# A two-layer decoder trunk on one core: the order of the mixers' side work changed

## The chip, the core and the metric

The kernel runs on one NeuronCore of a Trainium2 chip. TensorE (PE) multiplies matrices and writes PSUM; VectorE (DVE), ScalarE (ACT) and GpSimd (POOL) do elementwise work; SyncE (SP) issues the transfers from HBM. Each engine works through its own instruction list strictly in order and waits for semaphores of the others. The metric is the device time of one execution in microseconds (us).

## The reference

A trunk of two layers over x of 256 × 2048, in fp32:

```python
# each layer, h = x @ w_in split by columns
y = concat(hgrn2(q, f, i, g), nsa(q, k_c, v_c, k_s, v_s, k_w, v_w, gate))
x = layer_norm(alpha * x + y @ w_out)
x = layer_norm(alpha * x + conv_ffn(x))        # w_up, causal conv of 3, silu gate, w_down

def compress(kv, pe, w1, w2):                  # of k_c and of v_c
    blk = kv[:, :, idx] + pe                   # 15 blocks of 32 positions, step 16
    return silu(flat(blk) @ w1) @ w2
# nsa: compressed, selected and sliding attention of 16 heads in 4 groups, summed with gates
# hgrn2: a gated linear recurrence of 8 heads with a state of 128 x 128, then RMS norm, gate
```

## The kernel before, in words

**Units.** All weights stream through one list of units (`run`). A unit is one transfer of 512 KB or 280 KB into one of 5 raw buffers, a split of each weight into a high part (whi, by ScalarE, or by GpSimd from the twentieth unit of a layer on: `POOL = 20`) and a low part (wlo = raw − whi, by VectorE), and matmuls. Transfers are issued up to 7 units ahead, splits are made up to 3 ahead, 4 buffers each for whi and wlo. A w_in or w_out unit is 8 blocks of two matmuls (512 columns with whi, 256 with wlo); a unit of w_vg, the values and gates of the selected and sliding branches, is 12 matmuls of 280 columns; a compression unit is 8 matmuls of 256 columns with w_c1 taken raw.

**The order of a layer's units** is written out in the mixer: three pairs of w_in columns (compressed, selected and window keys; `pairs(0, 3)`), the keys' eight vg units with a compression unit behind each two, the pair of the compressed values (vc), the same for the values, and then q, f, g and v units by a plan string, w_out, w_up, w_down.

**Side work.** Attention and the recurrence are generators in two queues, `att` and `hgr`. `pump` takes a step of one or the other after each unit. `cmp_in` (8 instructions of VectorE) lays out the compression's input from the keys or the values, plus a position term; `cmp_tail` does silu and the second product. Keys reach `cmp_in` through `total` (the sum of both halves in PSUM), a swap of halves (L400, 4 instructions) and two sums (L402, L403). The keys of the windows are also split for the scores, kh by ScalarE and kl by VectorE (L432). The scores of a query (L513) wait for its q, split at L413. `pre_att`, ahead of the first block of w_out, ends all that is left in the attention queue.

**What sets the final order.** A scheduler places the recorded instructions on each engine; the names end in numbers of buffers.

Of the kernel before, what the change touches and what calls it, by code (L numbers as in the profile page):

```python
# [29 lines left out]
F32 = mybir.dt.float32  # L30
# [11 lines left out]
KT = D // 128  # L42
# [23 lines left out]
VG = 280  # L66


def blocks(cts, nk, outer=0, head=0, tail=0):

    first, rest = cts[:outer], cts[outer:]
    if head:
        o = [(c, k) for c in first for k in range(head)]
        o += [(c, k) for c in first for k in range(head, nk)]
    else:
        o = [(c, k) for k in range(nk - tail) for c in first]
        o += [(c, k) for c in first for k in range(nk - tail, nk)]
    return o + [(c, k) for c in rest for k in range(nk)]  # L80
# [2 lines left out]
N_IN = 40  # L83
OUTER, TAIL = 6, 2
ORDER_IN = blocks(range(N_IN), KT, outer=OUTER, tail=TAIL)
ORDER_OUT = blocks(range(KT), KT, outer=3, head=12)
ORDER_UP = blocks(range(2 * FT), KT, outer=OUTER, tail=TAIL)
ORDER_DOWN = blocks(range(KT), FT)

# [3 lines left out]
RAW_BUFS, PART_BUFS = 5, 4  # L93
LOOK_DMA, LOOK_SPLIT = 7, 3
URGENT = 4
POOL = 20

AFTER = 3, 5, 6, 8, 9, 10, 12, 13, 14
# [5 lines left out]
class Trunk:  # L104
    def __init__(self, tc, a):
        self.tc, self.nc, self.a = tc, tc.nc, a
        self.side = self.att = deque()
        self.side2 = self.hgr = deque()
        self.n = 0
        self.scopes = {}  # L110
        self.barriers, self.last = deque(), None
        self.back = iter(())


    def nm(self, s):
# [24 lines left out]

    def pump(self, k):

        while k > 0 and (self.side or self.side2):
            q = self.side if self.side else self.side2
            try:
                next(q[0])
                k -= 1
            except StopIteration:
                q.popleft()
                continue  # L150
            self.side, self.side2 = self.side2, self.side
# [285 lines left out]
    def cmp_in(self, l, kv, src):  # L437


        F = self.scratch()[:, :960].rearrange("p (j n) -> p j n", j=16)  # L440
        pe = self.par[:, P_PE + 32 * kv:P_PE + 32 * kv + 32]
        for g in range(4):
            r = 64 * (g % 2)
            for hf in range(2):
                b = src[r:r + 64, g // 2, 16 * hf:16 * hf + 240].rearrange(
                    "p (n j) -> p j n", n=NCMP)
                self.nc.vector.tensor_add(  # L447
                    F[64 * hf:64 * hf + 64, :, g * NCMP:g * NCMP + NCMP], b,
                    pe[r:r + 64, 16 * hf:16 * hf + 16].unsqueeze(2).to_broadcast([64, 16, NCMP]))
        return F  # L450

    def cmp_tail(self, l, kv, ps):
        nc, mw, n = self.nc, self.mw, 4 * NCMP
        t2 = self.t(mw, [128, 2, S], F32, "rope2")
        hd, sg = t2[:, 0], t2[:, 1]
        nc.scalar.activation(hd[:n], ps[64:64 + n, :256], AF.Copy)
        nc.vector.tensor_add(hd[:n], ps[:n, :256], hd[:n])
        nc.scalar.activation(sg[:n], hd[:n], AF.Sigmoid)
        nc.vector.tensor_mul(sg[:n], hd[:n], sg[:n])
        hT = self.t(mw, [128, 128], F32, "AD")[:, :2 * n].rearrange("p (k n) -> p k n", k=2)  # L460
        pt = self.t(self.ps_t, [128, 512], F32, "t")
        for k in range(2):
            nc.tensor.transpose(pt[:, k * n:k * n + n], sg[:n, k * 128:k * 128 + 128],
                                self.ident[:n, :n])
        nc.scalar.activation(hT.rearrange("p k n -> p (k n)"), pt[:, :2 * n], AF.Copy)
        po = self.t(self.ps_s, [128, 512], F32, "s")
        if kv == 0:
            for k in range(2):
                nc.tensor.matmul(po[:, :n], self.par[:, P_W2K + k * 128:P_W2K + k * 128 + 128],
                                 hT[:, k], start=k == 0, stop=k == 1)  # L470
            pv = po[:, :n].rearrange("p (g n) -> p g n", g=4)
            nc.scalar.activation(self.kh[:, :, :NCMP], pv, AF.Copy)
            nc.vector.tensor_sub(self.kl[:, :, :NCMP], pv, self.kh[:, :, :NCMP].bitcast(F32))
        else:
            for g in range(4):
                for k in range(2):
                    r = 32 * (g % 2)
                    nc.tensor.matmul(po[r:r + NCMP, g * 64:g * 64 + 64],
                                     hT[:, k, g * NCMP:g * NCMP + NCMP],
                                     self.par[:, P_W2V + k * 64:P_W2V + k * 64 + 64],  # L480
                                     start=k == 0, stop=k == 1, skip_group_check=True)
            for h in range(2):
                src = po[32 * h:32 * h + NCMP, :256].rearrange("p (j c) -> p j c", j=2)
                for r in (32 * h, 64 + 32 * h):
                    nc.scalar.activation(self.vcmp[r:r + NCMP, :, self.gc(0, h)],
                                         src[:, :, self.gc(0, h)], AF.Copy)
# [229 lines left out]
    def hgrn_out(self, l, hp, g):  # L716
# [4 lines left out]
        for h in range(2):  # L721
            c = slice(256 * (hp % 2) + 128 * h, 256 * (hp % 2) + 128 * h + 128)
# [21 lines left out]
        for h in range(2):  # L744
# [1 line left out]
            v.scalar_tensor_tensor(ov[:, h], pt[:, h].rearrange("p t c -> p (t c)"),  # L746
                                   self.par[:, P_NW + hh:P_NW + hh + 1], g["g"][:, h],
                                   op0=ALU.mult, op1=ALU.mult)
        if hp > 1:
            self.open_o(4 + hp)  # L750
        o = self.o[4 + hp]
        act(o[:, :, 0], ov, AF.Copy)
# [262 lines left out]
    def open_mix(self):  # L1015
# [1 line left out]

        self.mo, self.o = mo, [None] * 8
        self.pad = self.t(mo, [128, 16], F32, "pad")
        for p in range(6):  # L1020
            self.open_o(p)
        self.P = (self.t(mo, [128, 2, 2, 2, 128], F32, "o6")[:, 0],
                  self.t(mo, [128, 2, 2, 2, 128], F32, "o7"))
# [15 lines left out]
    def layer(self, l):  # L1039
        a, nc = self.a, self.nc  # L1040
# [29 lines left out]
        def d_q(j, ip):  # L1070
            def f(t):
                q = self.q_in(t)
                for i in range(2):
                    self.att.append(self.attend(j, 2 * ip + i, q[:, i]))
            return f

        hg = [dict() for _ in range(4)]
# [43 lines left out]
        def cmp_units(kv):  # L1121
            st = {}
            out = []
            for c in range(4):
                def cb(raw, c=c):
                    if c == 0:
                        st["ps"] = self.t(self.ps_h, [128, 512], F32, "h")
                    F = box[f"F{kv}"]
# [4 lines left out]
                                         raw[:, k * 256:k * 256 + 256],  # L1133
                                         start=jj < 2, stop=jj > 13, skip_group_check=True)
                    if c == 3:
                        self.cmp_tail(l, kv, st["ps"])
                out.append((a["w_c1"][l, kv, c], 1024, False, cb, LOOK_SPLIT))
            return out

# [41 lines left out]
        def pairs(p, n=1):  # L1181
            return tiles[4 * p:4 * (p + n)]
# [1 line left out]
        def values(n):  # L1184
            return self.tok_units(lambda kq: a["w_v"][l, n, kq], 512, 2, d_hv(n), pump=2)

        u = pairs(0, 3)
        for br in range(2):
            if br:
                u += pairs(3)  # L1190
            vg = self.tok_units(lambda kq, br=br: a["w_vg"][l, br, kq], VG, 2, d_vg(br))
            for c, cu in enumerate(cmp_units(br)):
                u += vg[2 * c:2 * c + 2] + [cu]
        Q, F, G = 4, 8, 10
        for step in PLAN.split():
            n = int(step[1])
# [6 lines left out]
            else:  # L1203
# [1 line left out]

        u[POOL:] = [x + (True,) for x in u[POOL:]]
        u += self.units(lambda n: a["w_out"][l, n], ORDER_OUT, lambda k: self.o[k // 2][:, k % 2], KT, self.d_res(l, 0),
                        pre={(0, 0): pre_att, (0, 8): pre_hgr, (0, 12): pre_out}, last=KT - 1)
        u += self.units(lambda n: a["w_up"][l, n], ORDER_UP, xin, KT, self.d_ff(l),
                        pre={(0, 0): pre_up}, wide=OUTER, group=8)  # L1210
        u += self.units(lambda n: a["w_down"][l, n], ORDER_DOWN, lambda k: self.f[:, k], FT,
# [131 lines left out]
```

## Time and profile before

| | |
|---|---|
| three runs | 2509.39, 2510.86, 2510.89 us; median 2510.86 |
| the profiled execution | 2509.09 us |
| its span, first to last instruction | 2507.3 us |
| PE, DVE, ACT, POOL busy | 98%, 71%, 48%, 17% |
| matmuls of w_in, w_up, w_down, w_out | most of PE's time |
| transfers | 432 MB read, 173 GB/s over the span |

PE is the engine that sets the span: what does not make PE wait costs nothing. A wait in the views below is idle time of an engine, with the instruction that ended it. Two of PE's matmuls that follow without a wait start a fixed time apart, so a stretch's own work can be counted from such starts.

### The profile page before, as it was taken

Reading aid. Unit: us, or ns where it says so; the run is one execution under the profiler, and the core shown is the slowest. Engines: PE = TensorE matmul, PEld = TensorE weight load, DVE = VectorE, ACT = ScalarE, POOL = GpSimd, SP = SyncE. Lnnn points to the kernel's source line nnn. Section 1 sums busy time; section 2 is a strip of 40 time slices with the busy share of each in tenths; the row PEclk is TensorE's granted clock in tenths of the full one; section 3 lists DMA queues with packets and bytes.
Section 4 is the critical chain, followed back from the end, with each engine's and each line's share of the span. In section 5 each row is a group of like instructions: output and inputs, shape, how many; then the busy total and the mean of one; then the engine's idle time right before and its main releaser. Section 6 shows DMA issues by size and latency. Waiting matters only on the chain.

```text
span 2507.3 us, 41290 instructions
## 1 busy us (share of the span) xinstructions
PE 2451.8 (98%) x15993; PEld 2116.0 (84%) x15993; DVE 1780.8 (71%) x2705; ACT 1196.0 (48%) x2189; POOL 428.0 (17%) x403
## 2 busy tenths in 40 slices
PE   8999999999999999999989999999999999999997
PEld 7788877888888888888878888788888888888887
DVE  7767876787777777555597678766977777775554
ACT  4144425465555555334331444354655555553443
POOL 0444551300000000001014445513000000000011
PEclk9999999999999999999999999999999999999999
DMA  6644343556666555566546443445556565566562
GB/s 236 213 155 142 119 145 124 184 163 193 192 193 190 190 192 192 187 193 193 160 155 204 159 135 124 139 134 177 174 190 192 192 191 189 192 187 197 181 201 101
DMA packets 122884, 436.99 MB, mean 174 GB/s; under 512 B 13760, under 2 KB 14528, under 8 KB 122688
## 3 DMA queue, kind: packets, MB, share of 16 engines
q1 hardware_dynamic: 122688, 434.35, 54.0%
q8 instruction: 126, 2.06, 0.3%
q14 instruction: 70, 0.57, 0.1%
HBM read 432.20 MB, written 2.10 MB: 173 GB/s over the span
## 4 chain that ended last, share of the span: by engine, by line
PE 86%; DVE 8%; issue 2%; POOL 1%; ACT 1%; DMA 1%; SPq 0%; ACTq 0%; POOLq 0%; DVEq 0%
PE pj L325 49%; PE pj L328 26%; DVE wlo L238 3%; PE pj L322 1%; PE t L325 1%; DVE rope L400 1%; PE pj L365 1%; PE pj L364 1%; PE pj L363 1%; PE h L657 1%; DVE sg L447 1%; PE s L592 1%; POOL whi L235 1%; DMA raw<-w_in 1%; PE s L513 1%
## 5 line engine op out<-in xcount | busy, mean ns | idle before, releaser
L238 DVE TENSOR_TENSOR wlo<-raw,whi 128x1024 fp32r<-128x1024 f32 (+2 forms) x819 | 1019.3, 1246 | 534.9 <-ACT whi L237 447.0
L325 PE MATMUL pj<-x,whi 128*128 128x512 f32 x3904 | 1117.6, 395 | 8.5 <-ACT whi L237 4.6
L237 ACT ACTIVATE whi<-raw 128x1024 fp32r<-128x1024 f32 (+2 forms) x631 | 661.9, 1049 | 788.8 <-PE pj L325 598.3
L325 PEld LDWEIGHTS pj<-x,whi 128*128 128x128 f32 x3904 | 709.0, 188 | 139.7 <-ACT whi L237 4.6
L328 PE MATMUL pj<-x,wlo 128*128 128x256 f32 x3904 | 715.6, 281 | 2.6 <-DVE wlo L238 2.5
L328 PEld LDWEIGHTS pj<-x,wlo 128*128 128x128 f32 x3904 | 592.2, 188 | 38.1 <-DVE wlo L238 4.0
L325 PE MATMUL pj<-f,whi 128*128 128x512 f32 x1320 | 329.7, 392 | 0.0
L235 POOL TENSOR_SCALAR whi<-raw 128x1024 fp32r<-128x1024 f32 (+1 forms) x188 | 218.1, 1162 | 329.3 <-PE pj L325 122.9
L325 PEld LDWEIGHTS pj<-f,whi 128*128 128x128 f32 x1320 | 235.9, 188 | 40.6
L828 POOL TENSOR_TENSOR s<-z 128x512 f32<-128x512 f32 x4 | 6.8, 1706 | 1179.3 <-DVE z L825 1179.3
L328 PEld LDWEIGHTS pj<-f,wlo 128*128 128x128 f32 x1408 | 188.0, 188 | 13.6
L328 PE MATMUL pj<-f,wlo 128*128 128x256 f32 x1408 | 192.9, 278 | 0.0
L1000 DVE SCALAR_TENSOR_TENSOR ct<-ch,par,ct 128x255 f32<-128x255 f32 (+1 forms) x352 | 168.0, 481 | 5.6
L325 PE MATMUL pj<-o,whi 128*128 128x512 f32 x480 | 169.9, 396 | 1.9 <-DVE o L600 1.9
L328 PE MATMUL pj<-o,wlo 128*128 128x256 f32 x512 | 144.1, 283 | 0.0
L325 PEld LDWEIGHTS pj<-o,whi 128*128 128x128 f32 x480 | 90.1, 188 | 23.8 <-DVE o L600 2.4
L998 ACT ACTIVATE ct<-ch,par 128x256 f32<-128x256 f32 x176 | 103.0, 588 | 0.0
L328 PEld LDWEIGHTS pj<-o,wlo 128*128 128x128 f32 x512 | 96.2, 188 | 0.4
L364 PE MATMUL pj<-wlo,x 128*128 128x280 f32 (+1 forms) x256 | 90.9, 356 | 4.9 <-DVE wlo L238 4.8
L363 PE MATMUL pj<-whi,x 128*128 128x280 f32 (+1 forms) x256 | 89.7, 357 | 2.7 <-POOL whi L235 2.7
L365 PE MATMUL pj<-whi,x 128*128 128x280 f32 (+1 forms) x256 | 90.5, 356 | 0.0
L375 DVE TENSOR_TENSOR ch<-pj,ch 128x256 f32<-128x256 f32 x170 | 70.9, 418 | 3.0 <-ACT ch L374 3.0
(248 smaller groups left out, 2244.8 us busy)
## 6 DMA issues: line engine op xcount, KB each, us to landing
raw<-w_up SPq DMA_DIRECT2D x352, 512.0 KB, 4.3
raw<-w_down SPq DMA_DIRECT2D x176, 512.0 KB, 4.1
raw<-w_in SPq DMA_DIRECT2D x158, 512.0 KB, 3.8
raw<-w_out SPq DMA_DIRECT2D x64, 512.0 KB, 3.6
raw<-w_v SPq DMA_DIRECT2D x32, 512.0 KB, 3.8
raw<-w_vg SPq DMA_DIRECT2D x32, 280.0 KB, 3.0
raw<-w_c SPq DMA_DIRECT2D x16, 512.0 KB, 3.6
out<-z SPq DMA_DIRECT2D x3, 512.0 KB, 2.6
```

Of the source, the lines that this page charges most:

```text
L235: self.nc.gpsimd.tensor_scalar(hi, raw, 1.0, 0.0, op0=ALU.mult, op1=ALU.add)
L237: self.nc.scalar.activation(hi, raw, AF.Copy)
L238: return self.nc.vector.tensor_sub(lo, raw, hi.bitcast(F32))
L322: mm(out[:, 0], hi[:, o], x[:, p], start=k == 0 and p == 0, stop=False, skip_group_check=True)
L325: mm(out, hi[:, o], x, start=k == 0, stop=False, skip_group_check=True)
L328: mm(st[c][:, 0], lo[:, 128 * i:128 * i + 128], act(k)[:, 0], start=False, stop=k == nk - 1, skip_group_check=True)
L363: mm(st[tt], xh, wh, start=first, stop=False, skip_group_check=True)
L364: mm(st[tt], xh, wl, start=False, stop=False, skip_group_check=True)
L365: mm(st[tt], xl, wh, start=False, stop=kt == KT - 1, skip_group_check=True)
L375: self.nc.vector.tensor_add(out, ps[:, 0], out)
L998: act(t[:, c], h[:, c], AF.Identity, scale=w[2], bias=w[3])
L1000: v.scalar_tensor_tensor(t[:, c, s:], h[:, c, :S - s], w[n], t[:, c, s:], op0=ALU.mult, op1=ALU.add)
```

## The change

Five edits, all to the mixers. (1) The pair vc comes directly behind the other three pairs; the vg and compression units of the keys and of the values then follow each other without a break. With that the twentieth unit of a layer, from which GpSimd splits, is the keys' fourth vg unit. (2) `cmp_in` of the values writes a buffer with the tag "o5" instead of the scratch that the keys' input uses; the sixth attention output, which has that tag too, is opened later. (3) `cmp_tail` is a generator: its first step runs at once, the rest is queued in `att` and may start two ticks (calls of `pump`) later. (4) An attention job put into an empty queue may start six ticks later. (5) The first three columns of w_out are taken in blocks of six, six and four tiles, and `pre_att` stands ahead of the seventh tile.

```diff
@@ -66,14 +66,13 @@
-def blocks(cts, nk, outer=0, head=0, tail=0):
+def blocks(cts, nk, outer=0, head=(), tail=0):
     if head:
-        o = [(c, k) for c in first for k in range(head)]
-        o += [(c, k) for c in first for k in range(head, nk)]
+        o = [(c, k) for a, b in zip((0, *head), (*head, nk)) for c in first for k in range(a, b)]
     else:
@@ -83,7 +82,7 @@
 ORDER_IN = blocks(range(N_IN), KT, outer=OUTER, tail=TAIL)
-ORDER_OUT = blocks(range(KT), KT, outer=3, head=12)
+ORDER_OUT = blocks(range(KT), KT, outer=3, head=(6, 12))
 ORDER_UP = blocks(range(2 * FT), KT, outer=OUTER, tail=TAIL)
@@ -93,6 +92,7 @@
 URGENT = 4
+DELAY = 6
 POOL = 20
@@ -110,6 +110,7 @@
         self.back = iter(())
+        self.ticks, self.due, self.kept = 0, {}, []
@@ -140,8 +141,14 @@
+        self.ticks += 1
+        early = lambda q: bool(q) and self.due.get(id(q[0]), 0) > self.ticks and k < 1 << 10
         while k > 0 and (self.side or self.side2):
-            q = self.side if self.side else self.side2
+            if early(self.side) and not self.side2 or early(self.side2) and not self.side:
+                return
+            q = self.side if self.side and not early(self.side) else self.side2
+            if not q or early(q):
+                return
             try:
@@ -437,7 +444,8 @@
-        F = self.scratch()[:, :960].rearrange("p (j n) -> p j n", j=16)
+        F = (self.t(self.mo, [128, 1024], F32, "o5") if kv else self.scratch())[:, :960]
+        F = F.rearrange("p (j n) -> p j n", j=16)
         pe = self.par[:, P_PE + 32 * kv:P_PE + 32 * kv + 32]
@@ -450,6 +458,7 @@
     def cmp_tail(self, l, kv, ps):
         nc, mw, n = self.nc, self.mw, 4 * NCMP
@@ -457,12 +466,14 @@
         nc.vector.tensor_mul(sg[:n], hd[:n], sg[:n])
+        yield
         hT = self.t(mw, [128, 128], F32, "AD")[:, :2 * n].rearrange("p (k n) -> p k n", k=2)
         nc.scalar.activation(hT.rearrange("p k n -> p (k n)"), pt[:, :2 * n], AF.Copy)
+        yield
         po = self.t(self.ps_s, [128, 512], F32, "s")
@@ -746,7 +757,7 @@
                                    op0=ALU.mult, op1=ALU.mult)
-        if hp > 1:
+        if hp > 0:
             self.open_o(4 + hp)
@@ -1017,7 +1028,7 @@
         self.pad = self.t(mo, [128, 16], F32, "pad")
-        for p in range(6):
+        for p in range(5):
             self.open_o(p)
@@ -1071,7 +1082,12 @@
                 for i in range(2):
-                    self.att.append(self.attend(j, 2 * ip + i, q[:, i]))
+                    job = self.attend(j, 2 * ip + i, q[:, i])
+                    if not self.att:
+                        self.due[id(job)] = self.ticks + DELAY
+                        self.kept.append(job)
+                    self.att.append(job)
             return f
@@ -1133,7 +1149,11 @@
                     if c == 3:
-                        self.cmp_tail(l, kv, st["ps"])
+                        job = self.cmp_tail(l, kv, st["ps"])
+                        next(job)
+                        self.att.append(job)
+                        self.due[id(job)] = self.ticks + 2
+                        self.kept.append(job)
                 out.append((a["w_c1"][l, kv, c], 1024, False, cb, LOOK_SPLIT))
@@ -1184,10 +1204,8 @@
-        u = pairs(0, 3)
+        u = pairs(0, 4)
         for br in range(2):
-            if br:
-                u += pairs(3)
             vg = self.tok_units(lambda kq, br=br: a["w_vg"][l, br, kq], VG, 2, d_vg(br))
@@ -1205,7 +1223,7 @@
         u += self.units(lambda n: a["w_out"][l, n], ORDER_OUT, lambda k: self.o[k // 2][:, k % 2], KT, self.d_res(l, 0),
-                        pre={(0, 0): pre_att, (0, 8): pre_hgr, (0, 12): pre_out}, last=KT - 1)
+                        pre={(0, 6): pre_att, (0, 8): pre_hgr, (0, 12): pre_out}, last=KT - 1)
         u += self.units(lambda n: a["w_up"][l, n], ORDER_UP, xin, KT, self.d_ff(l),
```

TensorE at the keys' compression in layer 0, before (h is the compression's sum, sg the laid-out input, pj_106 and pj_107 the two halves of vg):

```order
L363 MATMUL pj_106_545<-whi_121_628,x_7_73 128x280
L363 MATMUL pj_107_546<-whi_121_628,x_7_73 128x280
L1132 MATMUL h_112_579<-raw_72_351,sg_97_470 60x256 x4
L1132 MATMUL h_112_579<-raw_93_437,sg_97_470 60x256 x4
L1132 MATMUL h_112_579<-raw_108_559,sg_97_470 60x256 x4
L364 MATMUL pj_106_545<-wlo_122_629,x_7_73 128x280
L365 MATMUL pj_106_545<-whi_121_628,x_7_73 128x280
```

And now, from the first compression on, and then from the third on (pj_121 and pj_122 are the halves of vg):

```order
L370 MATMUL pj_121_648<-whi_124_664,x_7_73 128x280
L1148 MATMUL h_127_682<-raw_97_478,sg_96_469 60x256 x4
L1148 MATMUL h_127_682<-raw_112_590,sg_96_469 60x256 x4
L371 MATMUL pj_121_648<-wlo_125_665,x_7_73 128x280
L372 MATMUL pj_121_648<-whi_124_664,x_7_73 128x280
```

```order
L1148 MATMUL h_127_682<-raw_123_662,sg_96_469 60x256 x4
L1148 MATMUL h_127_682<-raw_131_705,sg_96_469 60x256 x4
L370 MATMUL pj_122_649<-whi_109_567,x_7_73 128x280
L371 MATMUL pj_122_649<-wlo_110_568,x_7_73 128x280
L372 MATMUL pj_122_649<-whi_109_567,x_7_73 128x280
```

The second half of vg, which used to alternate with the first, now stands behind all four compressions and writes pj_122.

VectorE there, before (hz and rope are the keys in work, kl the low part of the window keys):

```order
L447 TENSOR_TENSOR sg_97_470<-hz_96_455,par_75_357 64x16x15 x8
L238 TENSOR_TENSOR wlo_122_629<-raw_111_577,whi_121_628 128x560
L432 TENSOR_TENSOR kl_28_128<-rope1_99_485,kh_27_127 64x2x2x128 x2
L238 TENSOR_TENSOR wlo_125_647<-raw_113_584,whi_124_646 128x560
L432 TENSOR_TENSOR kl_28_128<-rope1_99_485,kh_27_127 64x2x2x128 x2
L375 TENSOR_TENSOR rope1_101_515<-t_40_153,rope1_101_515 128x256
L375 TENSOR_TENSOR rope1_101_515<-t_41_156,rope1_101_515 128x256
L400 TENSOR_TENSOR rope2_102_524<-rope1_101_515,cf32_77_361 32x512 x4
L238 TENSOR_TENSOR wlo_129_671<-raw_119_620,whi_128_670 128x1024
```

And now (h_127 is the sum of the keys' compression, pj_107 one half of the compressed values):

```order
L410 TENSOR_TENSOR rope1_100_488<-rope1_100_488,rope2_101_497 128x512
L455 TENSOR_TENSOR sg_96_469<-hz_95_454,par_74_356 64x16x15 x8
L245 TENSOR_TENSOR wlo_125_665<-raw_108_565,whi_124_664 128x560
L439 TENSOR_TENSOR kl_27_127<-rope1_100_488,kh_26_126 64x2x2x128 x4
L382 TENSOR_TENSOR rope1_102_518<-t_39_152,rope1_102_518 128x256
L382 TENSOR_TENSOR rope1_102_518<-t_40_155,rope1_102_518 128x256
L407 TENSOR_TENSOR rope2_103_527<-rope1_102_518,cf32_76_360 32x512 x4
L409 TENSOR_TENSOR rope1_102_518<-rope1_102_518,cf32_76_360 128x512
L410 TENSOR_TENSOR rope1_102_518<-rope1_102_518,rope2_103_527 128x512
L439 TENSOR_TENSOR kl_27_127<-rope1_102_518,kh_26_126 64x2x2x128 x4
L466 TENSOR_TENSOR rope2_149_818<-h_127_682,rope2_149_818 60x256
L382 TENSOR_TENSOR rope1_111_587<-pj_107_548,rope1_111_587 128x256
```

The splits (wlo) that stood between the kl instructions are gone from there; the sum from the keys' compression and the total of the compressed values (pj_107) stand behind the window keys instead.

TensorE at the start of w_out in layer 0, before (t_681 turns the recurrence's output, t_702 the last attention job's probabilities):

```order
L325 MATMUL pj_718_4584<-o3_21_119,whi_697_4473 128x512
L328 MATMUL pj_718_4584<-o3_21_119,wlo_698_4474 128x256
L739 MATMUL t_681_4381<-cf32_77_361,rope2_679_4372 128x128 x4
L572 MATMUL t_702_4480<-cf32_77_361,P0_640_4130 128x128
L573 MATMUL t_702_4480<-cf32_77_361,P1_639_4129 128x128
```

And now (s_677 are scores, t_673 turns the recurrence's output, s_685 collects an attention job):

```order
L548 MATMUL s_677_4334<-cb_77_362 128x288
L750 MATMUL t_673_4315<-cf32_76_360,rope2_671_4306 128x128 x4
L594 MATMUL t_678_4349<-cf32_76_360,Pc_32_134 128x128
L600 MATMUL s_685_4393<-rope2_656_4213,vcmp_34_136 128x256
L603 MATMUL s_685_4393<-PT_654_4211,v_28_128 64x256 x2
L606 MATMUL s_685_4393<-PT1_655_4212,v_28_128 64x128 x2
```

Before, the w_out blocks ran up to the last transposes and collect. Now scores, transposes of the recurrence and a collect (t_673, s_685) stand ahead of the last w_out blocks of the head.

## Rows read from the trace of the kernel before

**Rows 1.** The page, busy time of each engine, its share, instructions.

```profile
PE 2451.8 (98%) x15993; PEld 2116.0 (84%) x15993; DVE 1780.8 (71%) x2705; ACT 1196.0 (48%) x2189; POOL 428.0 (17%) x403
```

**Rows 2.** PE's waits, 40 to 110 us: line, releaser, us, times, longest.

```profile
PE pj L328 <- DVE wlo L238: 2.2, 1, 2.2
```

**Rows 3.** PE's waits, 355 to 425 us.

```profile
PE pj L325 <- DVE o L600: 0.9, 1, 0.9
PE s L589 <- ACT rope L586: 0.6, 1, 0.6
PE t L572 <- DVE hg L746: 0.6, 1, 0.6
```

**Rows 4.** Stretches: length; PE, PEld, DVE, ACT, POOL busy; PEclk, DMA share, GB/s.

```profile
362.00:367.00 5.00, 4.30 (x12) 3.18 (x13) 3.79 (x7) 1.08 (x2) 0.00 (x0) 0.66 0.48 161
...
1298.00:1319.00 21.00, 17.08 (x76) 12.63 (x77) 19.62 (x25) 3.89 (x9) 6.10 (x6) 0.67 0.56 185
```

**Rows 5.** PE's timeline: start, us, engine, line, what it does.

```profile
41.03 0.29 PE L363 MATMUL pj<-whi,x 128*128 128x280 f32 x1
41.16 0.29 PE L364 MATMUL pj<-wlo,x 128*128 128x280 f32 x1
...
67.12 0.39 PE L325 MATMUL pj<-x,whi 128*128 128x512 f32 x1
...
67.47 0.39 PE L325 MATMUL pj<-x,whi 128*128 128x512 f32 x1
...
96.88 1.08 PE L1132 MATMUL h<-raw,sg 128*60 128x256 f32 x8
...
362.69 0.68 PE L513 MATMUL s<-kh,q 128*128 128x512 f32 x1 [3.89 <-DVE q L413]
...
1284.41 0.29 PE L363 MATMUL pj<-whi,x 128*128 128x280 f32 x1
...
1343.39 1.08 PE L1132 MATMUL h<-raw,sg 128*60 128x256 f32 x8
```

**Rows 6.** VectorE's and GpSimd's timeline, keys' compression of both layers.

```profile
43.57 2.77 DVE L400 TENSOR_TENSOR rope<-rope,cf 32x512 f32<-32x512 f32 x4
...
47.03 0.69 DVE L402 TENSOR_TENSOR hz<-hz,cf 128x512 f32<-128x512 f32 x1
47.63 1.39 DVE L238 TENSOR_TENSOR wlo<-raw,whi 128x560 fp32r<-128x560 f32 x2
...
50.74 5.04 DVE L447 TENSOR_TENSOR sg<-hz,par 64x240 f32<-64x240 f32 x8
...
56.47 1.38 DVE L432 TENSOR_TENSOR kl<-rope,kh 64x512 fp32r<-64x512 f32 x2
...
60.55 0.76 DVE L375 TENSOR_TENSOR rope<-t,rope 128x256 f32<-128x256 f32 x2 [0.51 <-ACT rope L374]
61.35 3.52 DVE L400 TENSOR_TENSOR rope<-rope,cf 32x512 f32<-32x512 f32 x4
...
1285.64 2.07 DVE L400 TENSOR_TENSOR hz<-hz,cf 32x512 f32<-32x512 f32 x3
...
62.57 1.06 POOL L235 TENSOR_SCALAR whi<-raw 128x1024 fp32r<-128x1024 f32 x1 [8.25 <-DMA raw<-w_in]
```

**Rows 7.** ScalarE's timeline; DMA issues: count, KB each, us to landing.

```profile
50.86 2.58 ACT L431 ACTIVATE kh<-rope 64x512 fp32r<-64x512 f32 x4 [5.60 <-DVE rope L403]
...
raw<-w_c SPq DMA_DIRECT2D x16, 512.0 KB, 3.6
```

**Rows 8.** VectorE and ScalarE at the last scores and the last collect.

```profile
361.95 1.40 DVE L413 TENSOR_TENSOR q<-rope,q 64x512 fp32r<-64x512 f32 x2
...
394.52 0.49 ACT L556 ACTIVATE P<-P,wg 128x256 f32<-128x256 f32 x1
...
401.12 0.28 ACT L732 ACTIVATE rope<-s 128x128 f32<-128x128 f32 x1 [1.59 <-PE s L725]
...
404.39 0.68 DVE L735 TENSOR_TENSOR rope<-s,hss 128x512 f32<-128x512 f32 x1
```

## The prediction

> **What bounds the kernel now.** I read the page's busy times first: TensorE (PE) is busy 98% of the span [rows 1]. A change of order can therefore only win or lose in the few places where PE waits, so the next view is PE's waits, stretch by stretch, then the granted clock there, then the timeline of the engine that PE waits for. The reader should see three places in each of the two layers. First, the stretch of the compressed keys and values, where PE waits for wlo splits and, in smaller pieces, for the compression's input (the largest in [rows 2]). I take its length from PE's own rows: it begins at 41.03 and its last compression matmul begins at 96.88 and runs about 1.0, so 56.9 us in layer 0; in layer 1 it is 1284.41 to 1344.4, 60.0 us [rows 5]. Second, the last query's scores: 3.9 us for one q [rows 5]. Third, the last collect of attention at the start of w_out: 0.9 + 0.6 + 0.6, 2.1 in all [rows 3]. The second and the third recur in layer 1 at the same size, by the same views.
>
> To the waits belongs the clock: granted 0.66 over 362–367 and 0.67 over 1298–1319 [rows 4], that is, pieces at 1.2 GHz instead of 2.4. In 362–367 that is 5.0 × 0.34/0.5 = 3.4 us at half rate, in which 1.7 us of work are lost. So the second place costs 3.9 + 1.7 = 5.6 us a layer.
>
> **The change, part by part.**
>
> *Scores later.* The first attend job put in an empty queue now waits six ticks. In the new order 22 w_v matmuls stand ahead of the last query's scores that stood behind them; at 0.23 each (512 columns at the rate of [rows 5], where a pair of 512 and 256 takes 0.35) that is 5.1 us of cover for a wait of 3.9. PE arrived at 362.69 − 3.89 = 358.8 [rows 5]; now it arrives at 363.9, and q is ready at 361.95 + 1.40 = 363.4 [rows 8]. The wait goes, and its half clock with it: −5.6 a layer. What is late next is the attend job itself: all that follows it comes later by as much, and its end meets w_out.
>
> *w_out on six tiles first.* In the order, 42 w_out matmuls (21 blocks) stood ahead of the last collect; 42 stand there now. The new head only changes which blocks these are, and adds no cover. But three chains now end between them. (i) The transposes t_673 need the scaled rows: squares on ScalarE, the reciprocal power on GpSimd, a multiply on VectorE. Before, that chain took from 401.12 to 404.39 + 0.68 = 405.07, 3.95 us [rows 8]. Between its last matmul and the transposes PE now has some 1.6 us of work (five w_out and six score instructions): a wait of 2.3. (ii) s_685 needs a copy that ScalarE issues behind three scalings of P of 0.4 to 0.5 each [rows 8], which wait for a softmax of the scores just before. Bounds: 0.6 (only the scalings, less PE's 0.7) to 2.6 (the softmax too); I take 1.7, in between. (iii) t_699 needs a second chain of 3.95, for which six w_out matmuls (1.05 us) are left: 1.8 to 2.9, I take 2.4. Sum 6.4. The closing collect keeps its 2.1. So 6.4 in place of 5.6: +0.8 a layer before the clock.
>
> *Compressed values early.* This moves the most. The four w_in units of the compressed values (vc) now stand ahead of the keys' vg and compression units; the buffer "o5" lets their cmp_in run at once instead of waiting for the scratch. PE's work is the same, VectorE's too; the question is in which order VectorE's list comes and where PE meets it. VectorE is done with the first two swaps at 43.57 + 2.77 = 46.3 [rows 6], and with a split of 1024 columns in place of one of 560 ahead of that, about 46.9. Then come a split of 1024 (1.2), three of 560 (0.7 each), four sums (0.60 each, 47.03 to 47.63): 52.5; the keys' cmp_in, 5.04: 57.5. PE has four units of eight blocks, 32 × 0.35 = 11.2, and 18 vg matmuls at 0.13 = 2.3: it is there at 54.5 and waits 3.0. Then PE does two compressions (2.0) and five vg matmuls. The third compression's weights can be issued only when a split ends at 58.2; the fourth's only when the third is over, because all five raw buffers are taken. At 3.6 us from issue to landing [rows 7] PE would do the fourth at 66.4, until 67.4. But the second halves of vg write the PSUM bank of the compressed values, and their total stands in VectorE's list behind the window keys: split 0.7, four kl 2.8, a copy waited for and two adds 0.5 + 0.8, swaps 2.8 to 3.5, sums 1.2, kh and the last kl 2.6 + 0.7, two adds 0.8 [rows 6, 7]: 57.5 + 13.3 = 70.8, the swaps taken at their middle. PE waits another 3.4; the late DMAs are covered by this. After that VectorE does the values' cmp_in (5.04), a product and a split (1.5 with the adds) ahead of the next vg unit: 77.3, for which PE has 24 × 0.13 + 0.3 = 3.4: a wait of 3.1. PE then has 142 vg matmuls and four compressions left, 22.5 us, and I leave 1.0 for the small waits of the splits there: 100.8 against 97.9, **+2.9**. In layer 1 the list starts later against PE: the swaps begin at 1285.64, 1.2 after PE's 1284.41, instead of 0.3 before it; 1.5 more on 59.8 is 61.3 against 60.0, **+1.3**. So the part that moves all of VectorE's compression ahead costs more than the wait for the scratch that it takes away. Below: if VectorE's list takes the shorter swaps and kh hides, −3; above, if the late DMAs come on top, +6 a layer.
>
> The row on the swaps: four take 2.77 at 43.57 with GpSimd idle and 3.52 at 61.35, while GpSimd splits from 62.57 on [rows 6]. The Trainium skill (GPSIMD Engine Reference, 1. Specifications) has GpSimd share its SBUF interfaces with VectorE and names VectorE instructions with two SBUF inputs as those that contend; the trace agrees with it. In the new order GpSimd takes over the splits from the keys' fourth vg unit on, and four of them fall beside the values' cmp_in, which has two such inputs. At 3.52/2.77, 27%, over all of its 5.04 that is +1.4 a layer, without contention 0; I take +0.5.
>
> The row on the clock: it fell to half in the pieces of [rows 4], in the first of them right after the wait of 3.9 [rows 5]. PE's new waits in this stretch are 3.0, 1.7, 3.6, 3.4 and 3.1. What PE does slowly before 70.8 is hidden by VectorE's list; behind the last wait it is not: 0 to 1.7 a layer, I take 1.0. At w_out, 6.4 of waits in some 12 us: 0 to 1.7, I take 1.0. The Trainium skill (TensorE: Matmul & The Clock Gate, Why this matters for your kernels) warns of idle gaps between bursts, after which the clock falls back to half; by it alone all four pieces would cost 1.7, +2.8 on the sum below.
>
> *Compression's tail as a job.* Its transposes keep their place in the order (behind four matmuls of the first q unit, before and now), so what PE waits there for VectorE stays: 0. If the due time does bring a cover, that wait goes, some 2 us a layer by the waits of its kind [rows 2].
>
> **The sum.** Layer 0 +2.9, layer 1 +1.3, port 2 × 0.5, clock 4 × 1.0, w_out 2 × 0.8: 2.9 + 1.3 + 1.0 + 4.0 + 1.6 = +10.8. The profiled execution took 2509.09, span 2507.3 with 1.8 around it; the median of the three runs is 2510.86. 2509.1 + 10.8 = 2519.9: I say 2520.
>
> **Rivals.** *Faster.* The new waits at w_out are hidden (ScalarE and GpSimd clear their chains while PE does the 42 w_out matmuls), so 5.6 goes twice with nothing back, and the compression comes out even: 2509.1 − 11.2 = 2498. For it: ScalarE is often idle there. Against it: the order puts each chain's end right before its user. *No change.* The list of VectorE comes out 3 shorter in layer 0 (the swaps at 2.77, kh hidden), the clock keeps up, and what the scores gain w_out takes: −0.1 + 1.3 + 1.6 = +3, 2509 to 2513. For it: VectorE's and PE's work is the same. *Worse.* The clock stays at half. In layer 1 it did: 21.0 × 0.33/0.5 = 13.9 us of 1298–1319 ran at half rate [rows 4]. If PE stays there for 6.8 us behind the split at 77.3, and as long at w_out, each piece costs 3.4 in place of 1.0: 10.8 + 4 × 2.4 = +20.4, 2529.5. It decides once the clock has not come back when PE has caught up with VectorE's list. Against it: in layer 0 full rate was back after 3.4 us in 362–367.
>
> **How the numbers follow.** What a measurement of this kernel can tell from no change is about 0.2%, 5 us, so slower begins at 2515.9. The forecast's kind (2514 to 2525) has 0.52; faster 0.13; no change 0.21; worse 0.14. Of the forecast's kind 0.02 lies under that bound. Faster 0.13, same 0.21 + 0.02 = 0.23, slower 0.50 + 0.14 = 0.64. The range leaves the outer half of the faster and of the worse rival out: 2504 to 2528; the forecast's own is 2514 to 2525.
>
> **What would show it.** Right: PE's wait for the last q gone in both layers; PE waiting some 3 us each for cmp_in, for the total of the compressed values and for the split behind the values' cmp_in; from PE's entry to the last value compression about 60 us in layer 0; three waits of 1.5 to 2.5 ahead of the last collect. Wrong: if that stretch is under 57 us, if the 42 w_out matmuls start with no wait between them, or if q's wait comes back elsewhere.

## The result

The changed kernel took 2529.14 us (median of 4 runs, 2528.46 to 2529.67) against 2510.88 of the kernel before on the same chip: a ratio of 1.0070 (95% interval 1.0058 to 1.0082). It is slower by 18.3 us, and 1.1 above the end of the predicted range. The direction was right, the size was not: +10.8 had been worked out.

The profiled execution's span is 2526.7 us, 19.4 more than before [rows 1]. In the busy times hardly anything shows:

```profile
PE 2459.8 (97%) x15993; PEld 2119.9 (84%) x15993; DVE 1776.0 (70%) x2705; ACT 1203.0 (48%) x2193; POOL 416.9 (16%) x401
```

PE works 8.0 us longer on the same 15993 instructions, which is work at the lower clock (windows below), and waits for the rest. Where, is read from four starts in PE's timeline of each kernel: the last matmul of the values' compression and the last of w_out, in both layers. The table gives how much longer each stretch was than in the kernel before (profiled executions; the stretches between w_out and the next layer differ by 0.0). The first column also holds PE's waits in the first 30 us of the program: 5.6 in the kernel before, 6.2 in the change, 5.0 to 5.8 in the others.

| run | to the last compression, layer 0 | from there to the end of w_out | layer 1: compression | w_out | sum | median, us | ratio to before (95%) |
|---|---|---|---|---|---|---|---|
| the change | +5.3 | +5.8 | +3.3 | +5.0 | +19.4 | 2529.1 | 1.0070 (1.0058–1.0082) |
| e1 values early | +4.7 | +1.7 | +3.2 | −0.4 | +9.4 | 2518.2 | 1.0024 (1.0015–1.0033) |
| e2 scores later, 6 | +0.5 | +7.9 | +0.1 | +8.0 | +16.5 | 2526.0 | 1.0056 (1.0044–1.0069) |
| e3 scores later, 4 | +1.4 | −3.5 | 0.0 | −2.8 | −5.0 | 2504.4 | 0.9971 (0.9960–0.9983) |
| e4 fill two waits | +5.7 | +5.1 | +3.3 | +5.9 | +20.0 | 2525.9 | 1.0058 (1.0044–1.0071) |
| e5 fill all waits | +5.7 | +0.5 | +3.1 | +3.1 | +12.4 | 2522.1 | 1.0042 (1.0030–1.0055) |
| e6 e1, GpSimd from 24 | +3.6 | −0.8 | +2.2 | −0.9 | +4.1 | 2514.7 | 1.0011 (1.0002–1.0020) |
| e7 the change, delay 4 | +5.4 | −4.1 | +3.2 | −3.0 | +1.4 | 2510.5 | 0.9995 (0.9986–1.0004) |
| e8 e3 with head and tail | +1.4 | −3.5 | −0.2 | −2.1 | −4.4 | 2504.5 | 0.9968 (0.9957–0.9980) |
| e9 e1, own tile | −2.9 | −1.3 | −5.1 | +0.3 | −9.0 | 2500.0 | 0.9953 (0.9940–0.9965) |
| e10 e7, own tile | −3.6 | −2.1 | −5.6 | −2.4 | −13.8 | 2494.5 | 0.9933 (0.9920–0.9945) |
| e11 e10, GpSimd from 24 | −4.5 | −1.8 | −6.6 | −3.4 | −16.2 | 2492.0 | 0.9923 (0.9910–0.9935) |
| e12 scores later, 5 | +2.2 | −4.7 | +0.7 | −3.5 | −5.3 | 2503.7 | 0.9969 (0.9957–0.9981) |

### The profile page after: what moved, and what is told of

It is laid out like the page before. It is cut to its first block, busy times and chain, and to the rows that moved or that the text cites. A ratio compares the mean times of both kernels' runs of the same rounds, so it can differ in the third digit from the quotient of the medians.

```text
span 2526.7 us, 41289 instructions
## 1 busy us (share of the span) xinstructions
PE 2459.8 (97%) x15993; PEld 2119.9 (84%) x15993; DVE 1776.0 (70%) x2705; ACT 1203.0 (48%) x2193; POOL 416.9 (16%) x401
## 4 chain that ended last, share of the span: by engine, by line
PE 88%; DVE 7%; issue 2%; ACT 1%; POOL 1%; DMA 1%; SPq 0%; ACTq 0%; POOLq 0%; DVEq 0%
PE pj L332 49%; PE pj L335 26%; DVE wlo L245 2%; PE pj L329 1%; PE pj L371 1%; PE pj L372 1%; PE t L332 1%; PE pj L370 1%; PE h L668 1%; DMA raw<-w_in 1%; PE s L603 1%; DVE rope L407 1%; PE t L335 1%; PE s L524 1%; PE h L332 1%
## 5 line engine op out<-in xcount | busy, mean ns | idle before, releaser
L242 POOL TENSOR_SCALAR whi<-raw 128x1024 fp32r<-128x1024 f32 (+1 forms) x186 | 209.6, 1128 | 337.7 <-PE pj L332 191.2
```

The source lines that it names most:

```text
L242: self.nc.gpsimd.tensor_scalar(hi, raw, 1.0, 0.0, op0=ALU.mult, op1=ALU.add)
```

## The profile after

PE's waits over 40 to 110 us (who waits, for whom, us, times, longest). Beside the split in [rows 2] the kernel before had

```profile
PE h L1132 <- issue: 1.8, 1, 1.8
PE pj L363 <- POOL whi L235: 1.7, 1, 1.7
PE t L463 <- DVE rope L459: 1.7, 1, 1.7
PE pj L364 <- DVE wlo L238: 1.5, 2, 1.1
PE h L1132 <- DVE sg L447: 0.7, 1, 0.7
```

and the change has

```profile
PE h L1148 <- DMA raw<-w_c: 3.7, 2, 3.5
PE pj L370 <- DVE rope L382: 2.8, 1, 2.8
PE h L1148 <- issue: 2.7, 1, 2.7
PE pj L371 <- DVE wlo L245: 0.8, 1, 0.8
```

These are the forecast waits for the fourth w_c transfer, for the values' total, for the keys' compression input (named "issue") and for the split. From 40 us to the last compression PE's waits add up to 8.0 before and 10.1 now, so they are 2.1 of the +5.3; 0.6 are the first waits of the program. The rest is work at the lower clock, without which PE would have waited longer for VectorE: 13.7 us of this stretch ran at 1.2 GHz in the change, 3.4 before. Over 355 to 425, where [rows 3] had 2.1 in all besides the last q's 3.9 (355 to 435 here):

```profile
PE t L750 <- DVE rope L746: 4.4, 2, 2.3
PE s L600 <- ACT rope L597: 1.7, 2, 0.9
PE s L524 <- DVE q L420: 1.3, 1, 1.3
PE pj L332 <- DVE o L611: 0.9, 1, 0.9
PE t L583 <- DVE hg L757: 0.6, 1, 0.6
```

The first row is the two transposes t_673 and t_699, the third the last query's scores, which still wait. PE's timeline with the same places, as in [rows 5]:

```profile
102.20 1.08 PE L1148 MATMUL h<-raw,o 128*60 128x256 f32 x8
...
368.85 0.51 PE L524 MATMUL s<-kh,q 128*128 128x512 f32 x1 [1.32 <-DVE q L420]
...
411.34 1.11 PE L750 MATMUL t<-cf,rope 128*128 128x128 f32 x4 [2.13 <-DVE rope L746]
...
413.54 0.79 PE L600 MATMUL s<-rope,vcmp 128*128 128x256 f32 x1 [0.87 <-ACT rope L597]
...
422.55 0.66 PE L750 MATMUL t<-cf,rope 128*128 128x128 f32 x4 [2.27 <-DVE rope L746]
```

In windows (columns as in [rows 4]; PEclk is the third number from the end) PE ran at the lower of its two levels in new places. The second and third are w_out in layer 0, the last is w_out in layer 1:

```profile
62.00:72.00 10.00, 3.46 (x18) 1.38 (x17) 8.66 (x15) 4.53 (x10) 0.00 (x0) 0.67 0.42 135
409.00:418.00 9.00, 6.00 (x28) 3.66 (x27) 4.53 (x18) 5.81 (x22) 1.21 (x2) 0.62 0.36 115
424.00:432.00 8.00, 5.98 (x28) 3.67 (x28) 1.39 (x4) 2.80 (x7) 0.00 (x0) 0.57 0.01 2
...
1666.00:1675.00 9.00, 7.18 (x38) 5.17 (x39) 3.46 (x12) 4.94 (x18) 0.00 (x0) 0.62 0.14 55
```

A mean of 0.62 over 9.00 us is 9 × 0.38/0.5 = 6.8 us at 1.2 GHz; the other two come to 6.9 and 6.8. Of each some 1.3 us is waiting, so about 5.6 us of slow work, of which 2.8 is lost: 5.6 in layer 0, 2.8 in layer 1. Over 362 to 367, where [rows 4] had 0.66, it ran at full rate now, and also behind the last q's wait, over 367 to 373.

VectorE, for [rows 6] and [rows 8]:

```profile
63.16 2.77 DVE L407 TENSOR_TENSOR rope<-rope,cf 32x512 f32<-32x512 f32 x4
...
68.07 2.79 DVE L439 TENSOR_TENSOR kl<-rope,kh 64x512 fp32r<-64x512 f32 x4 [0.69 <-ACT kh L438]
...
71.37 0.76 DVE L382 TENSOR_TENSOR rope<-pj,rope 128x256 f32<-128x256 f32 x2
...
74.98 2.77 DVE L455 TENSOR_TENSOR o<-rope,par 64x240 f32<-64x240 f32 x4
77.79 2.99 DVE L245 TENSOR_TENSOR wlo<-raw,whi 128x560 fp32r<-128x560 f32 x4
...
367.39 2.13 DVE L420 TENSOR_TENSOR q<-rope,q 64x512 fp32r<-64x512 f32 x2
```

The values' total comes at 71.4 behind the window keys (63.2 to 70.9), as forecast (70.8). The last q's split ends at 369.5, 6.2 later than before.

## The experiments

**One part alone.** e1 keeps of the change the early pair and the buffer o5:

```diff
-ORDER_OUT = blocks(range(KT), KT, outer=3, head=(6, 12))
+ORDER_OUT = blocks(range(KT), KT, outer=3, head=(12,))
-DELAY = 6
+DELAY = 0
...
+                        for _ in self.cmp_tail(l, kv, st["ps"]):
+                            pass
...
-                        pre={(0, 6): pre_att,
+                        pre={(0, 0): pre_att,
```

> The kernel before with only the compressed values early (their pair ahead of the keys' units, the input in o5); no later scores, no queued tail, the old head of w_out. Theory A (two separate losses, one in the compression and one at w_out): only the first, +5.3 in layer 0 and +3.2 in layer 1 as the whole change has them, so 2511 + 8.5 = 2519.5 (2518 to 2521), with waits of some 2.7, 3.5 and 2.8 in layer 0 and no new wait at w_out; the last scores keep their 3.9. Theory B (the compression's lateness alone makes the chains at w_out late): nearly the whole loss, 2527 or more. Theory C (the order of the compression costs nothing, all is lost at w_out): 2511.

Measured 2518.2, ratio 1.0024. The stretch of the compressions has nearly the whole loss of the change there (+4.7 and +3.2 of +5.3 and +3.3), with waits for the same two things:

```profile
PE h L1148 <- DMA raw<-w_c: 3.7, 2, 3.5
PE pj L370 <- DVE rope L382: 3.5, 1, 3.5
```

e2 keeps the delay alone (with e1's head and tail, and `pairs(0, 3)` with the values' pair behind the keys'), e3 is e2 with `DELAY = 4`:

> The kernel before with only the six ticks for the first attention job in an empty queue (values' input in o5 too, which changes no order of PE). Theory A: the last scores' wait falls from 3.9 to about 1.3, and the three chains at w_out bring waits of 2.1, 0.9 to 1.4 and 2.3 with two pieces at half clock: +5.9 and +5.0, 2521.9 (2520 to 2524). Theory B: without the late compression the chains find their place, 2505. Theory C: most of the loss, 2525 or more.

> As the last one, with four ticks in place of six. In the order some 19 w_v matmuls then stand ahead of the last query's first scores, 4.4 us of cover for 3.9, and the transposes and collects stand among the w_out matmuls where the kernel before has them. Theory A, in its form that the harm is in how late the last job ends and not in the waiting itself: the scores' wait and its half clock go in both layers and nothing comes at w_out, 2511 - 11 = 2500 (2499 to 2504). Rival: any tick of delay is given back at w_out, 2511 to 2520.

e2 measured 2526.0, ratio 1.0056: the delay alone costs 8 a layer at w_out. That is more than the 2520 to 2524 of its theory A, since the collect waits 2.6 there where it waits 0.9 in the change. So e1 and e2 together lose more than the whole change (+9.4 and +16.5 against +19.4). e3 measured 2504.4, ratio 0.9971: two ticks less, and it is faster than before by 7. The largest of PE's waits of e2 and then of e3, 355 to 435:

```profile
PE t L750 <- DVE rope L746: 4.3, 2, 2.3
PE s L600 <- ACT rope L597: 3.2, 2, 2.6
PE s L524 <- DVE q L420: 1.3, 1, 1.3
```

```profile
PE pj L332 <- DVE o L611: 0.9, 1, 0.9
PE s L600 <- ACT rope L597: 0.6, 1, 0.6
PE t L583 <- DVE hg L757: 0.6, 1, 0.6
PE s L524 <- DVE q L420: 0.3, 1, 0.3
```

With four ticks the last q's wait is all but covered and only the old closing waits are left at w_out; the clock is 1.00 over 360 to 425. In PE's order the last transposes of the recurrence have 24 w_out matmuls ahead of them with four ticks, 6 with six.

**The clock at w_out.** e4 gives PE work in two of the change's waits, e5 in all three and also ahead of the last collect (twelve matmuls each time, whose sums nothing uses):

```diff
+FILL = 12
...
+        if hp > 1:
+            for _ in range(FILL):
+                i = nc.tensor.matmul(pt.rearrange("p h t c -> p (h t c)")[:, :416], self.identb, self.cb, ...)
+                self.after(i, pw)
```

and in e5 also

```diff
+        if j == 1 and i > 1:
+            for _ in range(FILL):
+                d = mm(po[:, :416], self.identb, self.cb, start=True, stop=True, skip_group_check=True)
+                self.after(d, last)
```

> The whole change, and ahead of the transposes of the last two pairs of heads of the recurrence 12 matmuls more (bf16, 416 columns, written to the tile that the transposes then overwrite), 2.1 us at full rate each time, in the place of PE's two waits of 2.1 and 2.3 in each layer. Theory A with the clock as the larger part of the loss at w_out: the half-rate pieces of some 6.8 us after these waits go, 4 to 5.5 us a layer, so 2529.1 - 6 to - 10: 2519 to 2523, granted clock 1.0 over 411 to 431. Rival (the waits themselves are the loss, the slow clock hides under them): 2529 to 2531.

> The whole change, with twelve matmuls of 416 bf16 columns (0.17 us each, 2.1 us a group; their sums are never used) ahead of the transposes of the recurrence's last two heads pairs, as in the last run, and also ahead of the second product of the two last collects, so that PE works through all the three waits of w_out (2.13, 0.87, 2.27 in layer 0; 2.13, 1.43, 2.29 in layer 1). Nothing comes earlier by it. Theory (the loss at w_out that the waits do not account for is PE at half its clock after them, some 5 us in layer 0 and 4 in layer 1): no piece at half rate over 405 to 432 and 1662 to 1690 us, 4 to 5.5 less a layer than the whole change (2529.1), 2518 to 2522, ratio to before about 1.003 to 1.004. Rival (the waits themselves and what stands behind them are the loss; the clock only follows): the same chains end at the same time, and the filling costs what it fills: 2526 to 2531, ratio 1.006 to 1.008, whether or not the half-rate pieces are there.

e4 measured 2525.9, ratio 1.0058, and told nothing apart: the order of ScalarE changed with it, the wait for the collect's copy grew, and the half-rate piece moved behind that wait (0.57 over 413 to 421). Its timeline:

```profile
414.83 1.22 PE L601 MATMUL s<-rope,vcmp 128*128 128x256 f32 x2 [2.92 <-ACT rope L598]
```

e5 measured 2522.1, ratio 1.0042, 7.0 below the change (the two intervals do not overlap), although its edit only adds work. Its windows at w_out, layers 0 and 1, have no slow piece:

```profile
405.00:432.00 27.00, 25.44 (x176) 18.93 (x175) 13.28 (x29) 14.89 (x53) 2.41 (x4) 1.00 0.13 39
1655.00:1685.00 30.00, 28.43 (x193) 21.53 (x192) 14.52 (x30) 16.24 (x55) 2.41 (x4) 1.00 0.15 53
```

Layer 0 gets back 5.3, as the theory had it; layer 1 only 1.9, where 4 had been expected: it had one slow piece, not two. The four fillings of a layer take PE 8.4, where the waits in their places were 6.1 in layer 0 and 6.5 in layer 1. So the clock's share is at least some 7 of the 18.3, and the rival, that filling gives nothing back, falls. One thing more differs: in e5 twelve matmuls of the recurrence (1.3 us) stand ahead of the first collect, in the change behind it.

**Four and five ticks.** e7 is the whole change with `DELAY = 4`, e8 the same without the early values (`pairs(0, 3)`), e12 is e3 with `DELAY = 5`.

> The whole change with a delay of four ticks instead of six for an attention job put into an empty queue. Theory (the loss is in two independent parts, the compressed values' stretch, some 5 in layer 0 and 3 in layer 1, and the delay that carries the last attention jobs into w_out, 5.8 and 5.0; with four ticks the second is a gain of some 3 a layer, as experiment e3_scores_later_4 had it): before + 8 - 6 = 2511 to 2514, ratio 1.000 to 1.001. Rival (the early values also push the last jobs into w_out, or the new head needs the six ticks): 2518 to 2529, with waits of about 2 left ahead of the last collect.

> All of the change but the early values (their pair stays behind the keys' compression), with a delay of four ticks: the queued tail of the compression, the six-tile head of w_out, and the scores later. Theory (the head won back 2 to 3 us a layer in the whole change against the delay alone because jobs were late there; with four ticks nothing is late and it has nothing to win): as e3_scores_later_4, 2503 to 2506, ratio 0.997 to 0.998. Rival (the head takes cover away from the last collect): its three closing waits (0.62, 0.25, 0.64) grow by 1 to 2 a layer, 2507 to 2509; other rival (the head wins here too): 2499 to 2501.

> Only the delay of the attention job, five ticks instead of the four of e3_scores_later_4 (2504.4) and the six of e2_scores_later (2526.0). In the order one collect of an attention job stands in w_out, but the last transposes still have 20 w_out matmuls ahead of them, where with six ticks a whole job's scores stand there and only 6 are left ahead of each of the last two. Theory (the loss is a step: it comes when the last job's scores fall into w_out and the chains to the last transposes lose their cover): as with four ticks within 3, 2502 to 2508, ratio 0.996 to 0.999. Rival (each tick later costs its share, since the end of the attention moves by as much): half way, 2512 to 2518.

e7 measured 2510.5, ratio 0.9995, just under the 2511 to 2514 of its theory: the two losses are independent, and the two ticks alone are worth 18.6. e8 measured 2504.5, ratio 0.9968, as e3: the new head and the queued tail give nothing once the delay is right; with six ticks they gave 2 to 3 a layer (change against e2). e12 measured 2503.7, ratio 0.9969: with five ticks 20 w_out matmuls still stand ahead of the last transposes. The loss is a step between five and six, not a price for each tick.

**The compressed values.** e6 is e1 with the unit from which GpSimd splits moved along:

```diff
-POOL = 20
+POOL = 24
```

> Experiment e1_values_early (values' pair early and its own buffer, nothing else of the change; 2518.2, ratio 1.0024), with the unit from which GpSimd splits moved from the twentieth to the twenty-fourth, so that GpSimd takes over at the same vg unit as in the kernel before. Theory (VectorE's list decides the stretch: the values' total stands behind the window keys, and the split behind the values' compression input): the three waits of about 2.7, 3.5 and 3.5 in layer 0 stay, the time is that of e1 within 1.5 us, 2517 to 2520, ratio 1.002 to 1.003. Rival (GpSimd's splits beside VectorE's two-input instructions slow VectorE, or come late themselves): the swaps and the compression input get shorter and the time falls to 2511 to 2515, ratio 1.000 to 1.001.

Measured 2514.7, ratio 1.0011: the rival's number, though the intervals of e1 and e6 overlap. Its three waits stay (2.5, 3.4 and 2.6 the largest), as the theory had it, but VectorE is done earlier. The two halves of the values' input in e6, against 2.77 for the second half in the change above:

```profile
71.04 2.31 DVE L455 TENSOR_TENSOR o<-rope,par 64x240 f32<-64x240 f32 x4
...
73.72 2.30 DVE L455 TENSOR_TENSOR o<-rope,par 64x240 f32<-64x240 f32 x4
```

In the compressions' stretch that is 1.1 and 1.0 a layer, so a third of the loss at most is GpSimd's; e6 is also 2.5 shorter than e1 behind the compressions of layer 0, which is not explained here. Why does the values' total stand behind the window keys at all? The keys and the values pass through a tile of one tag, rope1, in a pool with one buffer of each tag (`open(name, bufs=1)`), so the total can't be written before the window keys have left it. e9 is e1 with another tile for the values, one that is free so early:

```diff
-        dones += [self.pair(w, self.pre_rope) for w in (d_k(0), d_k(1), d_vc)]
+        own = lambda: self.t(self.mw, [128, 2, S], F32, "hg", bufs=2)
+        dones += [self.pair(w, self.pre_rope) for w in (d_k(0), d_k(1))]
+        dones += [self.pair(d_vc, own)]
```

> Experiment e1_values_early (2518.2, ratio 1.0024) with one more edit: the sum of the values' two halves is written to a tile with the tag hg, which nothing else uses so early, instead of the single tile rope1 that the selected and the window keys pass through first. In VectorE's order the values' total and half of their compression input then stand ahead of the keys' input, the rest ahead of the window keys, and on PE 22 more vg matmuls (2.9 us) stand ahead of the first compression. Theory (the loss of the early values is this one shared tile: the values' total, and with it the second halves of vg and a split, wait for the window keys to leave it): PE's wait for the total (3.5 in layer 0, 2.3 in layer 1) is gone, that for the fourth transfer of w_c (3.5, 4.2) at least halved, the wait ahead of the first compression stays at 2 to 3; the stretch to the last compression 3 to 5 shorter in each layer than in e1, the time 2508 to 2513, ratio 0.999 to 1.001. Rival (VectorE has the same work to do wherever it stands, or the transfers decide): the waits move to the splits and the time is that of e1 within 2.

Measured 2500.0, ratio 0.9953: 18 below e1 and 11.6 below the kernel before, where 5 to 10 below e1 had been expected. In the table 7.6 and 8.3 of it lie in the two stretches of the compressions. VectorE's timeline now has both totals (hg) ahead of the window keys (rope<-t at 69.47):

```profile
51.73 0.41 DVE L382 TENSOR_TENSOR hg<-pj,hg 128x256 f32<-128x256 f32 x1
...
53.91 2.58 DVE L455 TENSOR_TENSOR o<-hg,par 64x240 f32<-64x240 f32 x4
56.50 5.01 DVE L455 TENSOR_TENSOR sg<-hz,par 64x240 f32<-64x240 f32 x8
...
62.21 0.42 DVE L382 TENSOR_TENSOR hg<-pj,hg 128x256 f32<-128x256 f32 x1
...
69.47 0.76 DVE L382 TENSOR_TENSOR rope<-t,rope 128x256 f32<-128x256 f32 x2
```

and PE's waits over 40 to 110 are for two things, where the change waited for four:

```profile
PE h L1148 <- DVE sg L455: 3.3, 1, 3.3
PE pj L371 <- DVE wlo L245: 1.4, 2, 0.8
```

The total's wait is gone, and so is that for the fourth w_c transfer, which now has 74 vg matmuls ahead of it where e1 has 24.

**Both mended.** e10 is e7 with e9's tile, e11 is e10 with `POOL = 24`.

> The whole change with a delay of four ticks (e7_change_delay4, 2510.5, ratio 0.9995) and the values' total in a tile of its own. Theory (both losses of the change are mended, and the two edits add up): 6 to 10 less than e7, 2500 to 2505, ratio 0.996 to 0.998, as fast as e3_scores_later_4 or a little faster. Rival (the shared tile is not what held the stretch): as e7 within 2, 2509 to 2513.

> The last kernel with GpSimd's first split at the twenty-fourth unit, as in e6_values_early_pool24. Theory (GpSimd's splits beside VectorE's compression input make that input longer, by about 1 a layer on PE's path in e1): 1 to 3 less than the last kernel. Rival (with the input off PE's path, GpSimd's help with the splits is worth more than what it slows): equal or up to 3 more.

e10 measured 2494.5, ratio 0.9933 (0.9920 to 0.9945), e11 2492.0, ratio 0.9923 (0.9910 to 0.9935): faster than the kernel before by 19.6, and than the change by 37. e10 is below the 2500 to 2505 of its theory, since e9's gain had been put too low. e11 is 2.5 below e10, within the 1 to 3 of its theory, but their intervals overlap; VectorE's keys' input takes 4.57 in e11, 5.01 in e10.

## Why the prediction was wrong

Step by step, in us a layer (layer 0 / layer 1; measured from the waits and windows above and the same views of layer 1):

| step | forecast | measured |
|---|---|---|
| compressions, with port and clock | +4.4 / +2.8 | +5.3 / +3.3 |
| last q: its wait | −3.9 | −2.6 / −2.6 |
| its half clock | −1.7 | −1.7 / −1.7 |
| three chains at w_out | +6.4 | +5.3 / +5.9 |
| clock at w_out | +1.0 | +5.6 / +2.8 |

The measured rows add up to 11.9 and 7.7, the table of runs has 11.1 and 8.3; the account is good to about 0.8 a layer.

*Compressions: right in their waits, and in part by luck in their sum.* The waits came as forecast (3.0, 1.7 + 3.6, 3.4, 3.1 against 2.7, 0.3 + 3.5, 2.8, 0.8), the total at 71.4 for 70.8. The last wait is short because PE, at half rate from 66 to 76, came late to it: there the slow clock did hide behind VectorE's list. Full rate was back at 76.5, before that split was ready, so the 1.0 taken for the clock behind it was not spent. Against it the split was ready at 78.9 for 77.3, and the port cost about 1.1 a layer where 0.5 had been taken (e6). What the step lacked is a reason: it took VectorE's order as given, and that order came from a shared tile (e9).

*Last q: mostly right.* 1.3 of its wait stays. The 5.1 of cover were counted against a q that is ready at a fixed time. PE came to the scores 8.7 later (367.5 for 358.8), but q was ready 6.2 later. 3.9 of that is the sum of its halves, which starts later; VectorE's timeline before and in the change:

```profile
349.29 0.41 DVE L375 TENSOR_TENSOR rope<-pj,rope 128x256 f32<-128x256 f32 x1
```

```profile
353.18 0.41 DVE L382 TENSOR_TENSOR rope<-pj,rope 128x256 f32<-128x256 f32 x1
```

The other 2.3 is VectorE's way from there: one more split (1.2) stands ahead of q's, and some instructions took about twice as long beside a split of GpSimd (the first half of q's split 1.41 against 0.69, GpSimd's at 366.96). It is not the late compressions: e2, which has them in time, waits the same 1.3.

*The tail: right.* Its wait stayed, 1.2 and 0.6 where it had been 1.7 and 1.0.

*The chains: right in place and size*, 6.4 forecast, 5.3 and 5.9 measured.

*The step that failed is the clock at w_out*: "At w_out, 6.4 of waits in some 12 us: 0 to 1.7, I take 1.0." The bound of 1.7 was the loss of the one piece of 362 to 367; layer 0 has two pieces, each twice as long. The kernel before had pieces of that length already: the 13.9 of 1298–1319 in [rows 4] are two, with full rate between them:

```profile
1298.00:1305.00 7.00, 6.18 (x28) 4.54 (x30) 6.79 (x11) 0.45 (x1) 0.18 (x1) 0.51 0.29 80
1305.00:1311.50 6.50, 4.05 (x31) 2.56 (x27) 5.88 (x8) 2.88 (x7) 2.84 (x3) 1.00 0.90 329
1311.50:1319.00 7.50, 6.86 (x21) 5.53 (x22) 6.95 (x8) 0.56 (x1) 3.08 (x3) 0.54 0.53 157
```

Of the 8.6 between 10.8 and 19.4 this term is 6.4 (4.6 and 1.8), the rest of q's wait 2.6, the compressions 1.4, less 1.6 for the chains, which is 0.2 too much. Here the clock hides behind nothing, since the chains of ScalarE and GpSimd start from what PE itself has just done. e5 bears it out: without the slow pieces 7.0 of the 18.3 are back.

The rival called worse had this mechanism, and it had been given 0.14 because full rate had come back after 3.4 us in [rows 4]. That its 2529.5 is so close to the 2529.1 measured is partly luck: of its four pieces the two behind the split did not come, and layer 0 has one more at w_out. One profile's piece was taken for the price of a piece. By the rule of the Trainium skill (TensorE: Matmul & The Clock Gate, Why this matters for your kernels) that gaps between bursts bring the clock down, the sum would have been 2522.7 with each piece at 1.7, as the prediction applied it. The trace differs from it: at w_out the clock fell in a wait of 2.1 followed by one of 0.9, shorter than the gaps that the section warns of, and a piece cost 2.8, not 1.7.

## What to carry to other kernels

Where a change puts new waits into a stretch without slack, price the clock behind each of them from the longest slow piece of the profile as well as from the mildest, and ask whether another engine's list hides it. Before taking a late producer's place in an order as given, look which buffer it writes: one shared tile cost this change 16 us (e7 against e10), and a delay two ticks too long 18.6 (the change against e7). A delay should be set to the wait that it covers, here four or five ticks, since with six the work landed where its own chains have no cover.

## What was not expected of the hardware

After one and the same wait of 3.89 us for the last q, PE ran at half rate for 3.4 us in the kernel before [rows 4], and for 6.8 in e1, layer 0 (10 × 0.34/0.5), as in e6 and e9; in layer 1 of these three it was 3.4 again:

```profile
366.00:376.00 10.00, 7.58 (x22) 5.55 (x23) 6.02 (x11) 4.01 (x10) 1.13 (x2) 0.66 0.31 105
```

So the slow piece behind a wait has no fixed price: the part of it that is work cost 1.7 in the one and some 3.0 in the other (0.7 of the 6.8 was still the wait). What decides between the two wasn't settled. Waits of 0.2 to 0.9, as the closing ones of e3 and e12, left the clock at 1.00 over 360 to 425.
